# Gated linear attentions on one Trainium2 core: queries of all heads decayed in one VectorE operation, level products as matmuls of each head's own rows

## The chip, the cores and the metric

The kernel runs on one core of a Trainium2 chip. The metric is device time in microseconds (us) of one execution. Engines are called PE (TensorE), DVE (VectorE), ACT (ScalarE), POOL (GpSimd) and SP (the queue that issues DMAs).

## The reference

The program is a forward pass of a small network over one sequence of 512 tokens of width 1024: two layers that each run four token mixers side by side, then one layer of each of two other kinds. The mixers that matter here are two gated linear attentions, "hgrn" (4 heads of 64 key channels) and "gla" (4 heads of 32), both of this function, in chunks of 64 tokens:

```
def chunk_gla(q, k, v, log_f):
    ...
    bc = jnp.cumsum(gc, axis=3)                    # decay, summed inside the chunk
    def step(state, inp):
        q_, k_, v_, b_ = inp
        diff = b_[:, :, :, None, :] - b_[:, :, None, :, :]
        decay = jnp.where(causal, jnp.exp(jnp.where(causal, diff, 0.0)), 0.0)
        attn = jnp.einsum('bhid,bhjd,bhijd->bhij', q_, k_, decay)
        ...
        o = (jnp.einsum('bhij,bhjv->bhiv', attn, v_)
             + jnp.einsum('bhid,bhdv->bhiv', q_ * jnp.exp(b_), state))
```

The decay differs from channel to channel, so `attn` is no plain product of q and k. The kernel builds it by levels: for m = 32, 16, 8, 4, 2, 1 a chunk falls into blocks of 2m tokens, and the pairs whose key lies in the lower half and whose query in the upper half of one block are a plain product, once both are decayed to the border between the halves. Each pair belongs to one level; the diagonal is done apart.

## The kernel before

`Net` records every operation of every engine through one helper, so each instruction in the trace has the line of that helper, L328, and is told apart by its tiles. The program is written as generators. `merge` (line 656) and `project` (891) interleave them: in each of the two layers (`layer1`, 1898) one stream carries the projections of the four mixers and of the memory's keys and values, and the mixers' cores (`gdn` 1536, `hgrn_core` 1241, `gla_mix` 1274, the latent attention "mla" 1396 to 1480) start inside it as their inputs come. Then `Plan` (from line 265) orders each engine's instructions anew. It is a list scheduler with prices (`cost`, 330), waits between engines and tile buffers that come free; what it writes is the fixed order of every queue. A change in one operation therefore also moves others. Tiles in PSUM have names of three kinds: psA (3 buffers, projections), psS (3 buffers, for nearly everything small: scores, transposes, states, level products) and psD (2 buffers). In SBUF, p4w is the ring of sixteen 128x1024 work tiles, p4p the mixers' inputs, "p" or p2 the ring of 128x512 tiles; wh and wl are the two halves of a split weight.

`gla_core` (1074) computes either linear attention. Channels lie on partitions: hgrn has W = 1024 columns, two heads on 128 partitions and two such sets (hp = 2, n2 = 2), gla W = 512 and four heads of 32 partitions (hp = 4, n2 = 1). For each level `decays(m)` (1093) makes E: two DVE subtractions of the summed decay, one Exp on ACT, one DVE multiplication of the lower halves by k, 128 rows at once. The queries go elsewhere, into Q, which has a 32-column block for each head: line r of the loop multiplies only head r's partitions into head r's block, the rest of Q is zero (two Q buffers, cleared on POOL at lines 1112 to 1114):

```
for r in range(hp):
    self.mul(Q[rows(r), :, r, :]..., g(E)[rows(r), :, :, 1, :], g(q)[rows(r), :, :, 1, :])
```

The product of a level (1159 to 1167) then takes one matmul for a chunk and set: stationary E, 128 channels by 64 keys, moving Q, 64 columns (hgrn) or 128 (gla). All go to one psS tile, and one `copy_predicated` of DVE writes the level's entries from it into AT. Six levels, then the products with the state and with v, and `finish` (1044): norm, gate, and transposes into the operand of the output projection.

Of the kernel before, what the change touches and what calls it, by code (L numbers as in the profile page):

```python
# [12 lines left out]
U32 = mybir.dt.uint32  # L13
# [6 lines left out]
S = 512  # L20
# [10 lines left out]
LEVELS = (32, 16, 8, 4, 2, 1)  # L31
# [582 lines left out]
class Net:  # L614
# [459 lines left out]
    def gla_core(self, q, k, b, v, dk, scale, out):  # L1074


        W = q.shape[1]
        n2 = W // S
        hp = 128 // dk
        ns = NT * n2  # L1080
        bv = lambda t, m: t.rearrange("p (x two m) -> p x two m", two=2, m=m)
        AT = self.p4()
        vv = v.rearrange("p (t h d) -> p t h d", t=NT, h=4)
        rows = lambda r: slice(r * dk, r * dk + dk)
        prow = lambda c: slice((c % 2) * 64, (c % 2) * 64 + 64)
        fcol = lambda j, c: slice(j * S + c * 64, j * S + c * 64 + 64)


        scol = lambda c, j: slice(((c // 2) * n2 + j) * 64, ((c // 2) * n2 + j) * 64 + 64)
        a3 = lambda t: t.rearrange("p (a d) -> p a d", d=64)  # L1090
        big = lambda: self.p4() if n2 == 2 else self.p2()

        def decays(m):


            E = big()
            bb, ee = bv(b, m), bv(E, m)
            ref = bb[:, :, 0, m - 1:m].broadcast_to([128, W // (2 * m), m])
            self.sub(ee[:, :, 0, :], ref, bb[:, :, 0, :])
            self.sub(ee[:, :, 1, :], bb[:, :, 1, :], ref)  # L1100
            self.act(E, E, AF.Exp)
            self.mul(ee[:, :, 0, :], ee[:, :, 0, :], bv(k, m)[:, :, 0, :])
            Q = Qs[len(done) % 2]
            done.append(m)
            g = lambda t: t.rearrange("p (g x two m) -> p g x two m", two=2, m=m, g=nc8)
            for r in range(hp):
                self.mul(Q[rows(r), :, r, :].rearrange("p g (x m) -> p g x m", m=m), g(E)[rows(r), :, :, 1, :],
                         g(q)[rows(r), :, :, 1, :])
            return E, Q

        nc8 = n2 * 8
        Qs, done = [self.p4([128, nc8, hp, 32]) for _ in range(2)], []
        for Q in Qs:
            self.G.memset(Q, 0.0)

        kd = big()
        b3 = b.rearrange("p (c j) -> p c j", j=64)
        self.sub(kd.rearrange("p (c j) -> p c j", j=64), b3[:, :, 63:64].broadcast_to([128, nc8, 64]), b3)
        self.act(kd, kd, AF.Exp)
        self.mul(kd, kd, k)  # L1120
        qk = big()
        self.mul(qk, q, k, self.G)
        el = self.st([128, nc8])
        self.act(el, b3[:, :, 63], AF.Exp)
        yield self.when(kd)
        kdt = self.p4([128, n2, NT, 128])
        for j in range(n2):
            ps = self.ps("S")
            for t in range(NT):
                self.tr(ps[:, t * 128:(t + 1) * 128], kd[:, j * S + t * 128:j * S + (t + 1) * 128])  # L1130
            self.act(kdt[:, j].rearrange("p t c -> p (t c)"), ps, AF.Copy)
        E, Q = decays(LEVELS[0])
        yield self.when(kdt, qk)

        ps = self.ps("S")
        for t in range(NT):
            for j in range(n2):
                self.mm(ps[:, (t * n2 + j) * hp:(t * n2 + j + 1) * hp],
                        qk[:, j * S + t * 128:j * S + (t + 1) * 128], self.heads[dk])
        dg = self.st([128, 16])  # L1140
        self.act(dg, ps[:, 0:16], AF.Copy)
        St = self.p4([128, 8, n2, 64])
        self.V.memset(St[:, 0], 0.0)

        us = [self.ps("S", [128, ns * 64]) for _ in range(2)]
        for c2 in range(4):
            for j in range(n2):
                for c in (2 * c2, 2 * c2 + 1):
                    for r in range(hp):
                        self.mm(us[c % 2][rows(r), scol(c, j)], kdt[prow(c), j, c // 2, r * dk:(r + 1) * dk],  # L1150
                                vv[prow(c), c // 2, j * hp + r, :])
        for c in range(7):
            for j in range(n2):
                self.stt(St[:, c + 1, j, :], St[:, c, j, :], el[:, j * 8 + c:j * 8 + c + 1],
                         us[c % 2][:, scol(c, j)], ALU.mult, ALU.add)
        diag = self.K["lev"][:, 6 * 64:7 * 64].unsqueeze(1).broadcast_to([128, 16, 64])
        self.mul(a3(AT), diag, dg.unsqueeze(2).broadcast_to([128, 16, 64]), self.G)
        yield self.when(E, Q)
        for li, m in enumerate(LEVELS):
            ps = self.ps("S")  # L1160
            for c in range(8):
                for j in range(n2):
                    o0 = ((c // 2) * n2 + j) * hp * 32
                    self.mm(ps[prow(c), o0:o0 + hp * 32], E[:, fcol(j, c)], Q[:, j * 8 + c].rearrange("p r q -> p (r q)"))
            up = lambda t: t.rearrange("p (a x two m) -> p a x two m", two=2, m=m, x=32 // m)[:, :, :, 1, :]
            mask = up(self.K["lev"][:, li * 64:(li + 1) * 64].bitcast(U32)).broadcast_to([128, 16, 32 // m, m])
            self.V.copy_predicated(up(AT), mask, ps.rearrange("p (a x m) -> p a x m", m=m, x=32 // m))
            if li + 1 < len(LEVELS):
                E, Q = decays(LEVELS[li + 1])
            else:  # L1170
                E = big()
                self.act(E, b, AF.Exp)
                self.mul(E, E, q)
            yield self.when(E)
        o = self.p4()
        ov = o.rearrange("p (a r d) -> p r a d", r=hp, d=64)
        for r0 in range(0, hp, 2):
            pss = [self.ps("S", [128, ns * 64]) for _ in range(2)]
            for c2 in range(4):
                for j in range(n2):  # L1180
                    for c in (2 * c2, 2 * c2 + 1):
                        for i in range(2):
                            self.mm(pss[i][prow(c), scol(c, j)], E[rows(r0 + i), fcol(j, c)], St[rows(r0 + i), c, j, :])
            for i in range(2):
                self.act(ov[:, r0 + i], a3(pss[i]), AF.Copy, scale=scale)
        for half in range(2):
            ps = self.ps("S")
            for c2 in range(half * 2, half * 2 + 2):
                for h in range(4):
                    for c in (2 * c2, 2 * c2 + 1):  # L1190
                        a0 = (c2 * 4 + h) * 64
                        o0 = ((c2 - half * 2) * 4 + h) * 64
                        self.mm(ps[prow(c), o0:o0 + 64], AT[prow(c), a0:a0 + 64], vv[prow(c), c2, h, :])
            s = slice(half * 512, half * 512 + 512)
            self.stt(o[:, s], ps, scale, o[:, s], ALU.mult, ALU.add)
        out.append(o)
# [1323 lines left out]
```

## Time and profile before

| | |
|---|---|
| runs | 2051.95, 2046.83, 2048.59 us; median 2048.59 |
| profiled execution | 2043.82 us, span 2042.0 us, mean granted PE clock 0.989 |
| busy, share of the span | PE 96%, PE weight loads 81%, DVE 62%, ACT 47%, POOL 17% |
| PE records | 13254 (a float32 matmul leaves two, a float32r one or a transpose one) |
| the two mixer stretches | 107 to 310 us and 820 to 1035 us |

A duration in the rows is that of one instruction from its start to its end, and PE's matmuls overlap; what a matmul costs PE is the distance from one start to the next. A row of a timeline joins neighbours of one kind: its count is of records, and the start of the next row less its own start is what the group took. The number in brackets at a row's end is the idle time ahead of it and what ended it.

### The profile page before, as it was taken

Reading aid. Unit: us, or ns where it says so; the run is one execution under the profiler, and the core shown is the slowest. Engines: PE = TensorE matmul, PEld = TensorE weight load, DVE = VectorE, ACT = ScalarE, POOL = GpSimd, SP = SyncE. Lnnn points to the kernel's source line nnn. Section 1 sums busy time; section 2 is a strip of 40 time slices with the busy share of each in tenths; the row PEclk is TensorE's granted clock in tenths of the full one; section 3 lists DMA queues with packets and bytes.
Section 4 is the critical chain, followed back from the end, with each engine's and each line's share of the span. In section 5 each row is a group of like instructions: output and inputs, shape, how many; then the busy total and the mean of one; then the engine's idle time right before and its main releaser. Section 6 shows DMA issues by size and latency. Waiting matters only on the chain.

```text
span 2042.0 us, 33217 instructions
## 1 busy us (share of the span) xinstructions
PE 1963.9 (96%) x13254; PEld 1663.4 (81%) x13254; DVE 1265.9 (62%) x2313; ACT 955.0 (47%) x1721; POOL 356.8 (17%) x403
## 2 busy tenths in 40 slices
PE   6999999999999999999999999999999999999999
PEld 5888778888888878787788888888899988888787
DVE  7697883644442266879836444422548886558796
ACT  5763363433332246633634333322446663457782
POOL 3312121100000023112203000000323331105131
PEclk9999999999999999999999999999999999999999
DMA  5321224433332433301344333325331213331121
GB/s 159 99 71 36 71 67 164 117 100 93 94 102 93 155 108 93 76 23 55 94 150 119 93 94 102 93 93 175 114 83 49 77 62 114 126 91 53 62 73 62
DMA packets 231305, 191.88 MB, mean 94 GB/s; under 512 B 22224, under 2 KB 201072, under 8 KB 231152
## 3 DMA queue, kind: packets, MB, share of 16 engines
q1 hardware_dynamic: 231152, 189.77, 30.4%
q8 instruction: 104, 1.70, 0.4%
q14 instruction: 49, 0.40, 0.1%
HBM read 174.54 MB, written 15.20 MB: 93 GB/s over the span
## 4 chain that ended last, share of the span: by engine, by line
PE 80%; DVE 11%; ACT 3%; issue 2%; POOL 2%; DMA 1%; SPq 1%; DVEq 0%; ACTq 0%; POOLq 0%
PE psA L328 59%; PE psS L328 12%; PE psD L328 9%; DVE p4w L328 7%; DVE wl L328 1%; POOL st L328 1%; DVE p L328 1%; DVE st L328 1%; ACT p4w L328 1%; DVE p4p L328 1%; SPq L328 1%; ACT wh L328 1%; DVE p4h L328 0%; DMA p4p<-in_x_dram 0%; ACT p L328 0%
## 5 line engine op out<-in xcount | busy, mean ns | idle before, releaser
L328 PE MATMUL psA<-p4h,wh 128*128 128x512 f32 (+1 forms) x2144 | 626.0, 376 | 4.0 <-ACT p4h L328 2.6
L328 DVE TENSOR_TENSOR wl<-wr,wh 128x1024 fp32r<-128x1024 f32 (+5 forms) x290 | 336.6, 1165 | 392.2 <-ACT wh L328 386.8
L328 ACT CAST wh<-wr 128x1024 fp32r<-128x1024 f32 (+6 forms) x304 | 299.0, 990 | 474.8 <-PE psA L328 283.8
L328 PEld LDWEIGHTS psA<-p4h,wh 128*128 128x128 f32 x2144 | 392.6, 190 | 83.2 <-ACT p4h L328 4.4
L328 PE MATMUL psA<-p4h,wl 128*128 128x512 f32 (+1 forms) x1072 | 403.2, 377 | 1.5 <-DVE wl L328 1.5
L328 PE MATMUL psA<-wh,p4h 128*128 128x256 f32 (+1 forms) x1792 | 353.0, 290 | 2.1 <-DVE p4h L328 1.7
L328 PEld LDWEIGHTS psA<-wh,p4h 128*128 128x128 f32 x1792 | 284.0, 190 | 6.6 <-DVE p4h L328 2.3
L328 PE MATMUL psA<-wl,p4h 128*128 128x256 f32 (+1 forms) x896 | 259.8, 290 | 0.0
L328 POOL TENSOR_SCALAR st<-st 128x1 f32<-128x1 f32 (+4 forms) x108 | 40.0, 370 | 1139.1 <-ACT p4w L328 781.4
L328 PEld LDWEIGHTS psA<-p4h,wl 128*128 128x128 f32 x1072 | 203.9, 190 | 35.5 <-DVE wl L328 1.7
L328 PEld LDWEIGHTS psA<-wl,p4h 128*128 128x128 f32 x896 | 170.5, 190 | 1.6
L328 PE MATMUL psA<-wh,p4w 128*128 128x512 f32 (+1 forms) x540 | 159.5, 368 | 0.0
L328 ACT ACTIVATE p<-p 128x512 f32<-128x512 f32 (+2 forms) x174 | 88.1, 526 | 107.1 <-DVE p L328 105.9
L328 POOL TENSOR_TENSOR st<-st,c 128x1 f32<-128x1 f32 (+4 forms) x106 | 113.9, 1077 | 7.5
L328 PEld LDWEIGHTS psA<-wh,p4w 128*128 128x128 f32 x540 | 96.5, 188 | 18.4 <-issue 0.7
L328 ACT ACTIVATE p4w<-psA 128x256 f32<-128x256 f32 (+5 forms) x138 | 61.6, 451 | 101.9 <-PE psA L328 100.9
L328 PE MATMUL psS<-p4w,p4w 128*64 128x64 f32 (+9 forms) x800 | 98.1, 283 | 7.4 <-DVE p4w L328 7.3
L328 PE MATMUL psS<-consts,p4w 128*128 128x128 f32 (+1 forms) x448 | 71.0, 293 | 34.4 <-DVE p4w L328 18.8
L328 PE MATMUL psA<-wl,p4w 128*128 128x512 f32 (+1 forms) x270 | 98.4, 365 | 0.0
L328 PE MATMUL psS<-wh,p4w 128*128 128x512 f32 x300 | 97.4, 395 | 0.0
L328 DVE TENSOR_TENSOR p<-psA,p 128x512 f32<-128x512 f32 x54 | 37.3, 690 | 95.7 <-PE psA L328 94.2
L328 PEld LDWEIGHTS psS<-consts,p4w 128*128 128x128 f32 x448 | 55.1, 154 | 44.4 <-DVE p4w L328 17.1
(228 smaller groups left out, 3242.5 us busy)
## 6 DMA issues: line engine op xcount, KB each, us to landing
wr<-in_w_in_dram SPq DMA_DIRECT2D x44, 512.0 KB, 3.8
wr<-in_ffn_w_gate_dram SPq DMA_DIRECT2D x44, 512.0 KB, 3.8
wr<-in_ffn_w_up_dram SPq DMA_DIRECT2D x44, 512.0 KB, 3.9
wr<-in_ffn_w_down_dram SPq DMA_DIRECT2D x44, 512.0 KB, 3.5
wr<-in_w_out_dram SPq DMA_DIRECT2D x16, 512.0 KB, 4.4
wr<-in_a_w_in_dram SPq DMA_DIRECT2D x16, 512.0 KB, 3.8
wr<-in_b_w_in_dram SPq DMA_DIRECT2D x16, 512.0 KB, 3.9
p4w<-xd SPq DMA_DIRECT2D x12, 512.0 KB, 4.8
```

The source lines that it names most:

```text
L328: op.fn(*op.args, **op.kw)
```

## The change

`decays` multiplies the queries in place: the upper halves of E get q as the lower ones get k, 128 rows at once. Q, its clearing and its two buffers go. The level product is now taken for each head from that head's own partitions of E: stationary 64 or 32 channels by 64 keys, moving the 32 queries. Two heads at a time write to two psS tiles, and each head has its own `copy_predicated`.

```
-            self.mul(ee[:, :, 0, :], ee[:, :, 0, :], bv(k, m)[:, :, 0, :])
-            Q = Qs[len(done) % 2]
-            ...
-            for r in range(hp):
-                self.mul(Q[rows(r), :, r, :]..., g(E)[rows(r), :, :, 1, :], g(q)[rows(r), :, :, 1, :])
-            return E, Q
+            for i, f in enumerate((k, q)):
+                self.mul(ee[:, :, i, :], ee[:, :, i, :], bv(f, m)[:, :, i, :])
+            return E
...
-        Qs, done = [self.p4([128, nc8, hp, 32]) for _ in range(2)], []
-        for Q in Qs:
-            self.G.memset(Q, 0.0)
...
-            ps = self.ps("S")
-            for c in range(8):
-                for j in range(n2):
-                    o0 = ((c // 2) * n2 + j) * hp * 32
-                    self.mm(ps[prow(c), o0:o0 + hp * 32], E[:, fcol(j, c)], Q[:, j * 8 + c].rearrange("p r q -> p (r q)"))
...
-            self.V.copy_predicated(up(AT), mask, ps.rearrange("p (a x m) -> p a x m", m=m, x=32 // m))
+            for r0 in range(0, hp, 2):
+                pss = [self.ps("S", [128, ns * 32]) for _ in range(2)]
+                for c2 in range(4):
+                    for j in range(n2):
+                        for c in (2 * c2, 2 * c2 + 1):
+                            for i in range(2):
+                                x0 = (c2 * n2 + j) * 32
+                                e = E[rows(r0 + i), fcol(j, c)]
+                                self.mm(pss[i][prow(c), x0:x0 + 32].rearrange("p (x m) -> p x m", m=m), e, bv(e, m)[:, :, 1, :])
+                ...
+                for i in range(2):
+                    self.V.copy_predicated(up(AT, hp)[:, r0 + i], mask, pss[i].rearrange("p (a x m) -> p a x m", m=m, x=32 // m))
```

In the whole program the matmuls go from 11528 to 12008 (level products from 288 to 768), DVE's multiplications from 1121 to 1073 tensor-tensor operations, its predicated copies from 24 to 72, POOL's clearings from 40 to 32. The order of PE is the same but for the two mixer stretches. Three places follow.

PE, layer 0, one level product of gla in the middle of the stretch, before. psS_361 is the product's tile, p4w_266 is Q, p2_350 is E; psA are projections (the latent attention's values and 128x256 ones of later mixers), psD the products of gdn:

```order
L328 MATMUL psA_359_454<-p4w_336_431,wl340_435 128x512
L328 MATMUL psD_351_446<-p4w_231_326,p4w_107_202 64x64
L328 MATMUL psS_361_456<-p4w_266_361,p2_350_445 64x128
L328 MATMUL psD_351_446<-p4w_231_326,p4w_107_202 64x64 x3
L328 MATMUL psS_361_456<-p4w_266_361,p2_350_445 64x128 x7
L328 MATMUL psA_399_494<-wh276_371,p4h_17_112 128x256
```

The same engine and mixer after the change, one level (p2_369 is E, both operands):

```order
L328 MATMUL psS_368_463<-p2_350_445 64x32 x5
L328 MATMUL psS_380_475<-p2_369_464 64x32
L328 MATMUL psS_381_476<-p2_369_464 64x32
...
L328 MATMUL psS_382_477<-p2_369_464 64x32 x4
L328 MATMUL psA_432_527<-wl279_374,p4h_17_112 128x256
L328 MATMUL psA_432_527<-wh278_373,p4h_21_116 128x256
L328 MATMUL psA_467_562<-wh275_370,p4h_14_109 128x256
...
L328 MATMUL psS_383_478<-p2_369_464 64x32 x4
L328 MATMUL psS_382_477<-p2_369_464 64x32
L328 MATMUL psS_383_478<-p2_369_464 64x32
```

Heads 0 and 1 alternate between psS_380 and psS_381; of heads 2 and 3 four products of psS_382 go alone, then sixteen projection matmuls, then psS_383 and the rest.

PE, layer 0, end of the mixers, before: psA_524 is the last projection of gla's gate, psS_525 and psS_547 scores of the latent attention, psD and the other psS transposes:

```order
L328 MATMUL psA_524_619<-wh397_492,p4h_21_116 128x256
L328 MATMUL psS_525_620<-p4w_355_450,p4w_353_448 128x384
L328 MATMUL psS_525_620<-c49_144,c48_143 128x128
L328 MATMUL psD_532_627<-consts1_96,p2_513_608 128x128
L328 MATMUL psS_547_642<-p4w_355_450,p4w_353_448 128x512
L328 MATMUL psS_547_642<-c49_144,c48_143 128x128
L328 MATMUL psD_552_647<-consts1_96,p2_520_615 128x128 x2
L328 MATMUL psS_553_648<-consts1_96,p4w_325_420 128x128 x4
L328 MATMUL psS_555_650<-consts1_96,p4w_325_420 128x128 x4
```

The same place after, from the gate's last matmul (psA_510) to the next scores (psS_523):

```order
L328 MATMUL psA_510_605<-wh429_524,p4h_21_116 128x256
L328 MATMUL psS_511_606<-consts1_96,p4w_324_419 128x128 x4
L328 MATMUL psS_513_608<-consts1_96,p4w_324_419 128x128 x4
L328 MATMUL psS_515_610<-p4w_374_469,p4w_372_467 128x256
L328 MATMUL psS_515_610<-c49_144,c48_143 128x128
L328 MATMUL psD_520_615<-consts1_96,p2_501_596 128x128 x4
L328 MATMUL psS_563_658<-consts1_96,p4w_544_639 128x128 x4
L328 MATMUL psD_494_589<-consts1_96,p4w_435_530 128x128 x4
L328 MATMUL psS_564_659<-consts1_96,p4w_544_639 128x128 x4
L328 MATMUL psD_496_591<-consts1_96,p4w_435_530 128x128 x4
L328 MATMUL psA_521_616<-p4w_489_584,p4w_375_470 64x512
...
L328 MATMUL psS_523_618<-p4w_374_469,p4w_372_467 128x384
```

Before, 11 instructions stood between the gate and psS_555; after, 38 stand between the gate and psS_523: 28 transposes, one score product with its mask and eight products with values. psS_523 is the first of them that needs the buffer of psS_515.

ACT at the same place, before:

```order
L328 ACTIVATE p4p_194_289<-psA_524_619 128x256
L328 ACT_TABLE_LOAD
L328 ACTIVATE p4p_194_289<-p4p_194_289 128x1024
L328 ACTIVATE p4w_530_625<-psD_552_647 128x2x128
L328 ACTIVATE p4w_554_649<-psS_553_648 128x512
L327 ACT_TABLE_LOAD
L328 ACTIVATE p2_528_623,st_529_624<-psS_525_620,st_527_622 128x384
```

And after:

```order
L328 ACTIVATE p4p_192_287<-psA_510_605 128x256
L328 ACTIVATE p4w_512_607<-psS_511_606 128x512
L328 ACTIVATE p4w_514_609<-psS_513_608 128x512
L328 ACT_TABLE_LOAD
L328 ACTIVATE p4p_192_287<-p4p_192_287 128x1024
L328 ACTIVATE p2_490_585<-psD_520_615 128x256
L328 ACTIVATE p4w_495_590<-psD_494_589 128x512
L328 ACTIVATE p4w_540_635<-psS_563_658 128x4x128
L328 ACTIVATE p4w_541_636<-psS_564_659 128x4x128
L327 ACT_TABLE_LOAD
L328 ACTIVATE p2_518_613,st_519_614<-psS_515_610,st_517_612 128x256
```

In both the gate's activation (two table loads around it) stands ahead of the softmax that frees the scores' psS tile; after the change five more evacuations stand in that row.

## Rows read from the trace of the kernel before

**Rows 1.** Busy time by stretch: window, length, PE, PEld, DVE, ACT, POOL busy (instructions), granted PE clock, DMA share, GB/s. The first two long ones are the mixers of layers 0 and 1; the short ones lie inside them.
```profile
107.00:310.00 203.00, 190.03 (x2242) 162.03 (x2243) 169.82 (x347) 101.19 (x197) 43.39 (x42) 0.97 0.23 66
820.00:1035.00 215.00, 200.33 (x2336) 170.45 (x2335) 176.99 (x366) 107.52 (x204) 43.81 (x44) 0.96 0.23 67
...
156.00:160.00 4.00, 3.97 (x50) 3.60 (x50) 1.74 (x3) 0.00 (x0) 0.00 (x0) 0.57 0.01 4
292.50:299.50 7.00, 5.96 (x28) 4.87 (x28) 5.67 (x11) 3.95 (x10) 0.63 (x1) 0.51 0.05 18
```
**Rows 2.** PE, timeline (start, duration, records): a level product of hgrn and what follows it.
```profile
141.04 1.20 PE L328 MATMUL psS<-p4w,p4w 128*64 128x64 f32 x32
142.17 0.38 PE L328 MATMUL psA<-wh,p4h 128*128 128x256 f32 x1
```
**Rows 3.** PE, timeline: a level product of gla, and what follows it.
```profile
210.74 1.09 PE L328 MATMUL psS<-p4w,p 128*64 128x128 f32 x16
211.76 0.44 PE L328 MATMUL psS<-consts,p4w 128*128 128x128 f32 x2
```
**Rows 4.** PE, timeline: products of two heads in turn, whose operands lie on different halves of the partitions and whose results go to two psS tiles (64 partitions each, the chunk states), and what follows; then the same with 32 partitions each.
```profile
147.22 1.09 PE L328 MATMUL psS<-p4p,p4w 64*64 64x64 f32 x58
148.13 0.24 PE L328 MATMUL psD<-p4w,p4w 64*64 64x64 f32 x1
...
231.28 0.58 PE L328 MATMUL psS<-p4w,p 32*64 32x64 f32 x24
```
**Rows 5.** PE, timeline: matmuls with few moving columns (2 columns against 128 stationary ones; 32 against 32), each with the row after it.
```profile
143.09 1.62 PE L328 MATMUL psS<-consts,p4w 128*128 128x2 f32 x14
144.64 0.33 PE L328 MATMUL psS<-p4p,p4w 64*64 64x64 f32 x4
...
166.53 0.88 PE L328 MATMUL psD<-p,p4w 32*32 32x32 f32 x42
167.33 0.69 PE L328 MATMUL psS<-p4w,p4w 128*64 128x64 f32 x14
```
**Rows 6.** DVE, groups by form (count, busy us, mean ns): the query multiplications of hgrn and of gla, the key multiplications of hgrn and of gla, the predicated copies, and three reductions of psS tiles of falling width.
```profile
L328 DVE TENSOR_TENSOR p4w<-p4w,p4p 64x512 f32<-64x512 f32 x24 | 19.7, 821 | 0.2
L328 DVE TENSOR_TENSOR p4w<-p,p4p 32x256 f32<-32x256 f32 x48 | 23.2, 483 | 0.7
L328 DVE TENSOR_TENSOR p4w<-p4w,p4p 128x512 f32<-128x512 f32 x12 | 12.3, 1029 | 3.5 <-ACT p4w L328 3.4
L328 DVE TENSOR_TENSOR p<-p,p4p 128x256 f32<-128x256 f32 x12 | 6.6, 560 | 1.4 <-ACT p L328 1.4
L328 DVE COPY_PREDICATED p4w<-consts,psS 128x512 f32<-128x512 uint32 x24 | 21.9, 911 | 1.1 <-PE psS L328 0.7
L328 DVE TENSOR_REDUCE st<-psS 128x1 f32<-128x512 f32 x20 | 13.4, 680 | 0.2 <-PE psS L328 0.2
L328 DVE TENSOR_REDUCE st<-psS 128x1 f32<-128x256 f32 x52 | 20.9, 415 | 0.9 <-PE psS L328 0.7
L328 DVE TENSOR_REDUCE st<-psS 128x1 f32<-128x128 f32 x20 | 5.4, 280 | 0.1
```
**Rows 7.** PE, timeline of both layers: the matmuls inside the mixers' cores ahead of which PE stood idle longest until DVE had written a p4w tile (idle time in brackets).
```profile
154.54 0.42 PE L328 MATMUL psS<-p4w,p4w 128*64 128x64 f32 x6 [2.40 <-DVE p4w L328]
156.03 1.08 PE L328 MATMUL psD<-p4w,p4w 64*64 64x64 f32 x16 [1.08 <-DVE p4w L328]
208.20 0.99 PE L328 MATMUL psS<-p4w,p4w 64*64 64x64 f32 x22 [1.51 <-DVE p4w L328]
875.52 0.42 PE L328 MATMUL psS<-p4w,p4w 128*64 128x64 f32 x6 [1.50 <-DVE p4w L328]
877.01 1.12 PE L328 MATMUL psD<-p4w,p4w 64*64 64x64 f32 x16 [1.07 <-DVE p4w L328]
930.35 2.25 PE L328 MATMUL psS<-p4w,p4w 64*64 64x64 f32 x57 [1.52 <-DVE p4w L328]
```
**Rows 8.** DVE, timeline: the predicated copy that follows the product of the third group.
```profile
212.63 0.71 DVE L328 COPY_PREDICATED p4w<-consts,psS 128x512 f32<-128x512 uint32 x1
```
**Rows 9.** PE, timeline: the end of the mixers of layer 0, from the scores after the last gate projection on.
```profile
286.81 0.81 PE L328 MATMUL psS<-p4w,p4w 96*128 96x384 f32 x2
292.25 0.78 PE L328 MATMUL psS<-consts,p4w 128*128 128x128 f32 x4 [2.87 <-DVE p4w L328]
293.50 1.97 PE L328 MATMUL psS<-consts,p4w 128*128 128x128 f32 x8 [0.48 <-ACT p L328]
296.03 1.76 PE L328 MATMUL psD<-consts,p 128*128 128x128 f32 x7 [0.56 <-DVE p L328]
...
299.21 1.83 PE L328 MATMUL psA<-p4w,p4w 128*64 128x512 f32 x8
300.87 0.82 PE L328 MATMUL psA<-p,p4w 128*64 128x256 f32 x8
```
**Rows 10.** ACT, timeline: the same place, from the evacuation of the gate's last projection over its activation to the next evacuations.
```profile
287.96 0.38 ACT L328 ACTIVATE p4p<-psA 128x256 f32<-128x256 f32 x1
288.36 1.28 ACT L328 ACT_TABLE_LOAD   x1
289.65 1.06 ACT L328 ACTIVATE p4p<-p4p 128x1024 f32<-128x1024 f32 x1
290.88 0.59 ACT L328 ACTIVATE p4w<-psS 128x512 fp32r<-128x512 f32 x1
```

More of the change, by code (lines that the diff above doesn't have):

```diff
@@ L1101, in decays @@
             self.act(E, E, AF.Exp)
-            self.mul(ee[:, :, 0, :], ee[:, :, 0, :], bv(k, m)[:, :, 0, :])
-            Q = Qs[len(done) % 2]
-            done.append(m)
-            g = lambda t: t.rearrange("p (g x two m) -> p g x two m", two=2, m=m, g=nc8)
-            for r in range(hp):
-                self.mul(Q[rows(r), :, r, :].rearrange("p g (x m) -> p g x m", m=m), g(E)[rows(r), :, :, 1, :],
-                         g(q)[rows(r), :, :, 1, :])
-            return E, Q
+            for i, f in enumerate((k, q)):
+                self.mul(ee[:, :, i, :], ee[:, :, i, :], bv(f, m)[:, :, i, :])
+            return E
         nc8 = n2 * 8
-        Qs, done = [self.p4([128, nc8, hp, 32]) for _ in range(2)], []
-        for Q in Qs:
-            self.G.memset(Q, 0.0)
         kd = big()
@@ L1131, in gla_core @@
             self.act(kdt[:, j].rearrange("p t c -> p (t c)"), ps, AF.Copy)
-        E, Q = decays(LEVELS[0])
+        E = decays(LEVELS[0])
         yield self.when(kdt, qk)
@@ L1157, in gla_core @@
         self.mul(a3(AT), diag, dg.unsqueeze(2).broadcast_to([128, 16, 64]), self.G)
-        yield self.when(E, Q)
+        yield self.when(E)
         for li, m in enumerate(LEVELS):
-            ps = self.ps("S")
-            for c in range(8):
-                for j in range(n2):
-                    o0 = ((c // 2) * n2 + j) * hp * 32
-                    self.mm(ps[prow(c), o0:o0 + hp * 32], E[:, fcol(j, c)], Q[:, j * 8 + c].rearrange("p r q -> p (r q)"))
-            up = lambda t: t.rearrange("p (a x two m) -> p a x two m", two=2, m=m, x=32 // m)[:, :, :, 1, :]
-            mask = up(self.K["lev"][:, li * 64:(li + 1) * 64].bitcast(U32)).broadcast_to([128, 16, 32 // m, m])
-            self.V.copy_predicated(up(AT), mask, ps.rearrange("p (a x m) -> p a x m", m=m, x=32 // m))
+            for r0 in range(0, hp, 2):
[7 more added lines that the diff above has]
+                                self.mm(pss[i][prow(c), x0:x0 + 32].rearrange("p (x m) -> p x m", m=m), e, bv(e, m)[:, :, 1, :])
+                up = lambda t, n: t.rearrange("p (a r x two m) -> p r a x two m", two=2, m=m, x=32 // m, r=n)[:, :, :, :, 1, :]
+                mask = up(self.K["lev"][:, li * 64:(li + 1) * 64].bitcast(U32), 1)[:, 0].broadcast_to([128, ns, 32 // m, m])
+                for i in range(2):
+                    self.V.copy_predicated(up(AT, hp)[:, r0 + i], mask, pss[i].rearrange("p (a x m) -> p a x m", m=m, x=32 // m))
             if li + 1 < len(LEVELS):
-                E, Q = decays(LEVELS[li + 1])
+                E = decays(LEVELS[li + 1])
             else:
```

## The prediction

> **What bounds the kernel now.** I read the busy time by stretch first, since the change touches only the two mixer stretches, and the shares of the whole span mix them with 1500 us of dense projections. In both stretches PE is the fullest engine, 190.0 of 203 us and 200.3 of 215 us; DVE has 169.8 and 177.0, ACT and POOL are far below [rows 1]. So a microsecond taken from DVE is worth something only where PE stood waiting for it, and a microsecond of PE work added costs nearly a whole one. What PE leaves unused there is 13 and 15 us of idle time. A second loss hides in busy time: in some short stretches the granted clock is at about half, the lower of its two levels, 0.57 for 4 us and 0.51 for 7 us [rows 1]; the first comes behind idle times of 2.40 and 1.08 us [rows 7], the second behind one of 2.87 us [rows 9]. Next I looked in the timeline for the waits behind PE's idle time. The six longest inside the cores end on a DVE write and come to 9.08 us, 4.99 in layer 0 and 4.09 in layer 1 [rows 7]. The other place is the end of the mixers, 3.91 us in layer 0 [rows 9], and there ACT is what is late: the gate's activation with its table loads stands ahead of the softmax [rows 10].
>
> **PE's products.** Before, a level of hgrn takes 1.13 us for 16 matmuls up to the next start [rows 2], and one of gla 1.02 us for 8 [rows 3]; each holds one change of operand shape. Products of two heads in turn go faster: 29 matmuls in 0.91 us, 31 ns each, because two that read different partitions and write different psS tiles run side by side [rows 4]; those of 32 partitions, 12 in 0.58 us, are no slower than singles. I set a slot, one matmul or one such pair, at 60 ns, below 71 and 63 (the two groups of 64 columns divided out, with the change of shape still in them), and a change of shape at 0.1 us, between the 0.17 and 0.04 that then remain. Gla's old product is (1.02 - 0.1)/8 = 115 ns. Old products: 192 x 60 + 96 x 115 ns = 22.6 us. In the new order of PE I count, of 768 products, 284 neighbouring pairs and 200 that stand alone: 484 slots x 60 ns = 29.0 us. That is +6.4 us. Changes of operand shape along PE's order fall from 282 to 255: -2.7 us. Net **+3.7 us**.
>
> The new product has only 32 columns, and no row shows 64 stationary by 32 moving. Ends: if a slot fell to what 32 by 32 takes, (0.80 - 0.1)/21 = 33 ns [rows 5], 484 slots make 16.0 us, net -9.3; if nothing ran side by side, 768 x 60 ns = 46.1 us, net +20.8. I take 60, since the row with 2 columns on 128 stationary ones shows that few columns alone do not make a matmul cheap: 7 matmuls in 1.55 us, 221 ns each [rows 5].
>
> A rule speaks against many small matmuls. The row shows 58 records starting in 0.91 us, 16 ns apart [rows 4], so 1536 records are not held back by their number, and the sum stays. The Trainium skill, "TensorE: Matmul & The Clock Gate", section "Wait — 56ns, not 53.3ns?", states that starts are never closer than about 25 ns however few the columns; by it the sum would have 1536 x 25 ns = 38.4 us for the new products, 9.4 us more, and a time of 2055; here the trace disagrees and decides, so this gets no chance of its own.
>
> **DVE and POOL.** Removed: 24 query multiplications of 64 rows and 48 of 32 rows, 19.7 + 23.2 = 42.9 us. Added: 12 and 12 of 128 rows, priced as the key multiplications of the same shapes, 12.3 + 6.6 = 18.9 us. The copies go from 24 to 24 of half and 48 of a quarter of the width. Scaled by the reductions of psS tiles (680, 415, 280 ns): 24 x 911 x 415/680 + 48 x 911 x 280/680 = 13.3 + 18.0 = 31.3 instead of 21.9 us, +9.4 [rows 6]. DVE: -42.9 + 18.9 + 9.4 = -14.6 us, some 7 in each layer. It is worth at most the 9.08 us of PE's waits on DVE [rows 7] and at least nothing, since behind most of them stands a chain (subtraction, exponential on ACT, multiplication, matmul) of which the query multiplication is one link, and the copy, another link, gets more numerous. I take half, **-4.5 us**. POOL's eight clearings fall away; POOL is idle four fifths of these stretches [rows 1], so nothing. No DMA is added; SP's queue stays.
>
> **The end of the mixers.** The new order puts other work between the gate's last projection and the next scores, on both engines. PE: 28 transposes at 0.12 us (8 in 1.97 us at half clock [rows 9], halved) = 3.4, a score and its mask an estimated 0.4, eight products with values 1.2 (2.41 us for the two groups at half clock [rows 9], halved): 5.0 us. ACT until the scores' buffer is free, in the order shown: 0.38 + 2 x 0.59 + 1.28 + 1.06 + 0.38 + 3 x 0.59 + 1.28 + 0.4 = 7.7 us [rows 10]. So PE waits about 2.7 us instead of 3.91: -1.2. The lower clock costs 3.4 us there now (7 us at 0.51 [rows 1]). A wait of 2.7 us is nearer to the 2.87 than to the 2.40 that cost half as much, so I give back nothing. Both layers: **-2.4 us**. Ends: nothing, or the whole 7.3 us twice, -14.6, if the waits go and the clock holds, since 24 of the memory's projection matmuls that stood behind this place now stand among its scores.
>
> **The sum.** +3.7 - 4.5 - 2.4 = -3.2 us. The profiled execution would go from 2043.82 to 2040.6; it lies 4.8 us under the median of the runs, 2048.59, and on that scale I forecast **2045.4 us**. About 0.3%, 6 us, is what a measurement here can tell from no change, so that is within it.
>
> **Rivals.**
> 1. Faster, 2033 us. Either the end of the mixers closes up (-14.6 instead of -2.4) or the 32-column slot is as short as 32 by 32 (-9.3 instead of +3.7); each alone gives about -15. For it: the memory's projections that now stand among the scores, and a short slot for few columns in [rows 5]. Against: ACT's row of five more evacuations, and the 221 ns.
> 2. Slower, 2057 us: psS runs out. There are three buffers, a product now takes two of them until DVE has copied both, and the next pair can start in one only. The copy of the product in [rows 3] ended 1.58 us after the last matmul [rows 8]; a quarter as wide, 1.25. Four products alone, 0.24 us, cover little, so a boundary costs 1.0 us where nothing else stands between. There are 24 inside gla (one in a level, one between levels, two layers); half of them bare gives +12. Against: in the place shown sixteen projection matmuls stand between; it decides where less than about 1 us of other PE work does. DVE, full to 84% of these stretches, can make the lag longer.
> 3. Slower, 2062 us: two heads' products do not run side by side when 32 columns wide; +20.8 instead of +3.7.
> 4. The change doesn't do what it says: hardly possible for the instruction counts, which are fixed; what can fail is only that PE's waits follow DVE's time, and then the forecast loses its 4.5 us and stays within no change (2050).
>
> **How the numbers follow.** The forecast with its own spread (the half of the waits, rival 4) 0.42, rival 1 0.29, rival 2 0.22, rival 3 0.07. Of the first, 0.32 lies within 0.3%, 0.08 faster, 0.02 slower. So faster 0.37, same 0.32, slower 0.31. Cases of both signs hold more than half, so the range has to take in 2033 and 2057 with a little at both ends for their prices: 2030 to 2061. The forecast's own range is 2040 to 2050.
>
> **What would show it.** Right: level products in pairs, 32 records in about 0.5 us where uncut; DVE's busy time about 15 us lower; copies near 0.55 and 0.38 us; idle time ahead of the first level products halved; PE waiting 2 to 3 us behind the gate and the clock near half after it. Wrong: level products with idle time ahead of them ended by a DVE write of AT, psS short (rival 2); pairs at 120 ns (rival 3); slots of 33 ns or a full clock at the end of the mixers (rival 1).

## The result: slower by 1.1%

The changed kernel took 2067.76 us (median of six runs, 2061.43 to 2077.17), the kernel before 2046.62 in the same comparison: ratio 1.0107, 95% interval 1.0076 to 1.0137. The time lies above the range that was given, and on the other side of no change from the forecast. Its profiled execution took 2067.0 us.

The page of the changed kernel, span and busy time of each engine:
```profile
span 2065.2 us, 35119 instructions
PE 1980.0 (96%) x14214; PEld 1677.2 (81%) x14214; DVE 1255.6 (61%) x2313; ACT 953.5 (46%) x1721; POOL 351.9 (17%) x395
```
PE stands idle for 85.2 us of the span, where it was 78.1 (2042.0 - 1963.9). So 7 of the 23 us of added span are idle time, and 16 are "busy" ones. The granted clock by stretch shows where these are: first the two mixer stretches, moved to their new places, then three short ones inside the level products (columns as in [rows 1]):
```profile
105.10:323.00 217.90, 199.55 (x2726) 171.61 (x2727) 161.71 (x345) 100.04 (x197) 40.95 (x40) 0.92 0.20 57
834.80:1058.00 223.20, 203.30 (x2803) 172.69 (x2802) 167.21 (x362) 105.46 (x202) 40.52 (x42) 0.93 0.20 57
199.80:206.60 6.80, 6.04 (x51) 5.51 (x55) 3.86 (x7) 1.95 (x5) 0.00 (x0) 0.50 0.19 60
230.50:233.90 3.40, 3.40 (x25) 2.25 (x26) 2.65 (x6) 1.78 (x3) 0.00 (x0) 0.50 0.00 0
237.30:251.00 13.70, 13.70 (x138) 12.68 (x138) 4.16 (x12) 2.62 (x6) 0.00 (x0) 0.50 0.23 77
```
The mixers' mean clock was 0.97 and 0.96 and is 0.92 and 0.93. At half clock PE is busy without a gap, 13.70 of 13.70 us: nothing but the column of the clock tells that the time is lost there. Over the span the mean clock is 0.979 instead of 0.989.

The sum over all stretches that the trace gives at half clock, before and after:
```profile
sum 46.16, PE 40.93 PEld 36.54 DVE 34.64 ACT 18.08 POOL 9.29; mean PE 4.55 PEld 4.06 DVE 3.85 ACT 2.01 POOL 1.03
sum 87.12, PE 75.45 PEld 64.04 DVE 52.48 ACT 29.88 POOL 14.75; mean PE 5.39 PEld 4.57 DVE 3.75 ACT 2.13 POOL 1.05
```
PE was busy at half clock for 75.4 us instead of 40.9. What that costs I estimate from two groups of the same 32 records further below: 1.05 us from start to next start at full clock, 1.85 at half, so 43% of the busy time at half clock is lost. That is 15 us more. Together with 7 us of idle time it leaves 1 us of the 23 for PE's own work, where the forecast had 3.7.

In uncut pairs the level products go as expected where the clock holds. PE, timeline of the changed kernel: a piece of a level of hgrn with the row after it, then gla:
```profile
177.83 0.85 PE L328 MATMUL psS<-p4w 64*64 64x32 f32 x46
178.62 0.44 PE L328 MATMUL psA<-wh,p4h 128*128 128x384 f32 x1
...
227.89 0.67 PE L328 MATMUL psS<-p 32*64 32x32 f32 x32
229.44 0.42 PE L328 MATMUL psS<-p 32*64 32x32 f32 x8 [0.88 <-DVE p4w L328]
```
Twenty-three matmuls in 0.79 us with one change of shape, 34 ns each: two run side by side in a slot of 60. The last row shows the other loss: PE stands for 0.88 us until DVE has written p4w. DVE at that time:
```profile
229.09 0.29 DVE L328 COPY_PREDICATED p4w<-consts,psS 128x128 f32<-128x128 uint32 x1
```
The copy ends at 229.38, the product starts at 229.44. Gla's products read E, a "p" tile; the p4w tile is AT, and nothing but the psS buffer ties a product to a copy of other heads. PE by form, over the whole span:
```profile
L328 PE MATMUL psS<-p 32*64 32x32 f32 x768 | 25.6, 236 | 6.3 <-DVE p4w L328 6.0
L328 PE MATMUL psS<-p4w 64*64 64x32 f32 x768 | 24.3, 225 | 8.4 <-DVE p4w L328 8.4
```
14.4 us of waits on DVE ahead of level products. DVE did get its relief; by form, the in-place multiplications and the copies:
```profile
L328 DVE TENSOR_TENSOR p4w<-p4w,p4p 128x512 f32<-128x512 f32 x24 | 28.1, 1206 | 9.8 <-ACT p4w L328 9.8
L328 DVE COPY_PREDICATED p4w<-consts,psS 128x128 f32<-128x128 uint32 x48 | 13.9, 349 | 17.5 <-PE psS L328 17.2
L328 DVE COPY_PREDICATED p4w<-consts,psS 128x256 f32<-128x256 uint32 x24 | 11.6, 531 | 0.5 <-PE psS L328 0.4
L328 DVE TENSOR_TENSOR p<-p,p4p 128x256 f32<-128x256 f32 x24 | 9.4, 418 | 2.9 <-ACT p L328 2.9
```
The copies take 531 and 349 ns, by count and mean 29.5 us in all (forecast 31.3); DVE's busy time falls by 10.3 us. The kernel got no faster by it.

### The profile page after: what moved, and what is told of

Read it like the earlier page. It is cut to its first block, busy times and chain, and to the rows that moved or that the text cites. A ratio compares the mean times of both kernels' runs of the same rounds, so it can differ in the third digit from the quotient of the medians.

```text
span 2065.2 us, 35119 instructions
## 1 busy us (share of the span) xinstructions
PE 1980.0 (96%) x14214; PEld 1677.2 (81%) x14214; DVE 1255.6 (61%) x2313; ACT 953.5 (46%) x1721; POOL 351.9 (17%) x395
## 4 chain that ended last, share of the span: by engine, by line
PE 78%; DVE 12%; ACT 4%; issue 3%; POOL 3%; DMA 1%; SPq 0%; DVEq 0%; ACTq 0%; POOLq 0%
PE psA L328 57%; PE psS L328 12%; PE psD L328 9%; DVE p4w L328 6%; POOL st L328 2%; DVE p L328 1%; DVE wl L328 1%; ACT p4w L328 1%; DVE st L328 1%; DVE p4p L328 1%; ACT wh L328 1%; ACT p L328 1%; SPq L328 0%; DMA wr<-in_w_in_dram 0%; DVE p4h L328 0%
## 5 line engine op out<-in xcount | busy, mean ns | idle before, releaser
L328 PE MATMUL psA<-wh,p4h 128*128 128x256 f32 (+1 forms) x1792 | 358.3, 294 | 2.2 <-DVE p4h L328 1.8
L328 PEld LDWEIGHTS psA<-wh,p4h 128*128 128x128 f32 x1792 | 289.1, 193 | 6.9 <-DVE p4h L328 2.3
L328 PE MATMUL psS<-p4w,p4w 64*64 64x64 f32 (+8 forms) x416 | 80.1, 314 | 2.3 <-DVE p4w L328 1.0
```

The source lines that it names most:

```text
L328: op.fn(*op.args, **op.kw)
```

## The experiments

Theory C: the granted clock falls more often, because the products by heads leave most of the array empty. Theory O: `Plan` prices a product at 81 ns, 62 us for the 768, where those in uncut pairs take 34 ns each; the order built on this puts products ahead of what they need. Rival W: waits for psS buffers and copies by themselves. The table gives every run; clock is the range over a kernel's runs. The last two columns are of one execution, the profiled one: idle is span less PE's busy time, half is PE's busy time in all stretches at half clock. That execution can lie far from the median: in e11 it took 2057.67 us, in e10 2049.50, in e12 2037.24.

| run | what | us | ratio to before (95%) | clock | PE idle us | PE half us |
|---|---|---|---|---|---|---|
| before | | 2046.62 | 1 | 0.985 to 0.991 | 78.1 | 40.9 |
| the change | | 2067.76 | 1.0107 (1.0076 to 1.0137) | 0.972 to 0.984 | 85.2 | 75.4 |
| e1_hgrn_only | change in hgrn alone | 2053.91 | 1.0041 (1.0027 to 1.0055) | 0.983 to 0.987 | 89.1 | 60.7 |
| e2_gla_only | change in gla alone | 2101.68 | 1.0272 (1.0255 to 1.0289) | 0.970 to 0.975 | 99.7 | 94.5 |
| e3_wide | 64 columns | 2067.56 | 1.0112 (1.0093 to 1.0130) | 0.979 to 0.982 | 85.3 | 70.8 |
| e4_price | price 31 ns | 2053.51 | 1.0033 (1.0011 to 1.0056) | 0.975 to 0.991 | 70.9 | 79.7 |
| e5_before_price | before, its prices as measured | 2046.08 | 0.9994 (0.9986 to 1.0003) | 0.985 to 0.989 | 79.9 | 54.4 |
| e6_gla_price | gla alone, 31 ns | 2068.56 | 1.0104 (1.0089 to 1.0120) | 0.972 to 0.974 | 75.2 | 113.6 |
| e7_price_full | 31 ns, full products | 2032.81 | 0.9937 (0.9922 to 0.9952) | 0.989 to 0.991 | 68.3 | 29.7 |
| e8_price_diag | 31 ns, diagonal on DVE | 2060.87 | 1.0063 (1.0042 to 1.0085) | 0.971 to 0.980 | 65.6 | 97.8 |
| e9_full | full products, the changed kernel's order | 2060.72 | 1.0067 (1.0045 to 1.0089) | 0.982 to 0.987 | 90.2 | 54.3 |
| e10_price_wide | 31 ns, 64 columns | 2040.14 | 0.9979 (0.9954 to 1.0004) | 0.978 to 0.991 | 69.6 | 66.9 |
| e11_hgrn_price | hgrn alone, 31 ns | 2041.67 | 0.9988 (0.9970 to 1.0005) | 0.980 to 0.989 | 78.3 | 76.2 |
| e12_hgrn_price_wide | the same, 64 columns | 2042.33 | 0.9977 (0.9966 to 0.9989) | 0.986 to 0.990 | 75.1 | 37.2 |
| e13_before_thin | before, one head's partitions | 2047.55 | 1.0011 (0.9997 to 1.0025) | 0.981 to 0.985 | 74.3 | 62.5 |
| e14_price_time | 31 ns as a time only | 2052.83 | 1.0032 (1.0015 to 1.0048) | 0.978 to 0.984 | 74.6 | 79.4 |
| e15_price_dense | 31 ns for the sparse rule only | 2062.02 | 1.0081 (1.0065 to 1.0097) | 0.983 to 0.986 | 82.1 | 50.2 |

Idle time and the 43% of the half column give the spans of the table to within some 3 us; in e1, e2, e8 and e15 some 7 to 10 us are left open.

**The change by halves.** The edit of both is a branch on the number of heads on 128 partitions, `if hp == 2:` (e1) or `if hp == 4:` (e2) around the new decays and products, the old ones in the other branch.

> The change in hgrn alone; gla keeps Q and its products of 128 rows. Theory C (the granted clock of PE falls more often where gla's small products stand, and that is most of the loss): 2048 to 2054 us, 0 to 6 over the kernel before, since the two longest added stretches at half clock (13.7 us from 237 us on, 10.2 us from 971 on) lie in gla's levels and only one of 6.8 us in hgrn's. Rival W (waits for psS and for DVE's copies): also most in gla, whose level takes two pairs of tiles, so 2049 to 2055, but with the clock unchanged at 0.988 and idle time ahead of the level products of 5 us or more. Rival O (the planner's new order as such, wherever it is disturbed): about half the loss, 2057.

> The change in gla alone; hgrn keeps Q and its products of 128 rows. Theory C: 2058 to 2066 us, a mean granted clock near 0.981, half clock inside gla's levels. Rival W: the same time with the clock near 0.988. Rival O: about half the loss, 2057.

Hgrn's 2053.91 us lie inside what C and W gave, but they are 9 us over the kernel before in the same comparison, more than C's 6, and the clock fell, against W. Gla alone costs 57, more than both changes together: no theory had that, and it shows that the parts do not add. A planner that writes the whole order makes a new one of every edit, which is what O says, though not by the half that I had put on it. In gla alone the idle time and the busy time at half clock both grow, by 22 and 54 us.

**The price.**
```
# Plan.cost                                  (e4_price)
+            if self.level(op):
+                return 0.031
# Plan.order                                 (e14_price_time adds / e15_price_dense has instead)
+            if op.eng == "PE" and self.level(op):
+                op.dense = self.columns(op) / 81.0        # e15: / 31.0, and no change in cost
```


> The changed kernel with one number of the planner altered: a level product is priced at 31 ns, half the measured slot of a pair, instead of 81 ns; the order changes by some 40 rows of PE. Rival O (the planner keeps a wrong account of the time that lies between the products, so that copies and products meet too early): 2050 to 2058 us. Theories C and W: 2062 to 2070 us, little changed.

> The planner uses a product's price twice: as the time it takes, and, divided into its columns, to call it sparse and put it back while it wants dense work. Here only the time is 31 ns; for the second use the changed kernel's number stays. If the wrong time is what cost 14 us: 2050 to 2056 us as with the altered price. If the second use is: 2064 to 2070 us.

> The other half: the time stays 81 ns, and only for the sparse rule the product counts as with 31 ns (hgrn's products are then not put back any more). If the wrong time cost the 14 us: 2062 to 2070 us as the changed kernel. If the sparse rule did: 2050 to 2056 us.

One number of the planner is worth 14 us of the 21, the time alone 15, the sparse rule alone 6, all three by medians: the twelve runs of e4_price spread from 2033.55 us (clock 0.991) to 2061.25 (0.975). Of the changed kernel's profile to that of e4_price the span falls by 12.3 us and the idle time by 14.3, while the busy time at half clock does not (75.4 and 79.7 us): the price saved waits, not clock. That a truer price does it, and not just another order, is argued and not shown: all three kernels that got 31 ns gained (e4, e6, e11), but no other number was tried for these products. PE by form in e4_price:
```profile
L328 PE MATMUL psS<-p 32*64 32x32 f32 x768 | 26.2, 246 | 0.0
L328 PE MATMUL psS<-p4w 64*64 64x32 f32 x768 | 22.6, 235 | 7.0 <-DVE p4w L328 7.0
```
With the same three psS buffers and the same copies gla's waits are gone, 0.0 instead of 6.0 us: W is real in the changed order, but it comes from the order.

> Control for the run with the altered price: the kernel before, its level products priced at their measured slots, 58 ns in hgrn and 108 in gla, instead of 81 and 135. Theory O' (the changed kernel lost because the planner's account of its products, 62 us where they take 25 to 29, is much farther off than that of the old ones, 28 us where they take 22): 2040 to 2048 us, no change. Rival (any truer price gives the 14 us): 2031 to 2036 us.

> The change in gla alone, which took 2101.7 us, with the price of its level products at 31 ns. Theory O': most of the 57 us goes, 2045 to 2060 us. Rival (gla's products by heads are slow by themselves: tiles, copies, clock): 2080 us or more.

> The change in hgrn alone (2053.9 us) with its level products priced at 31 ns. Theory (order built on a wrong price): 2040 to 2048 us, idle time in the mixers no more than before. Rival: hgrn's loss is its pairs of tiles, 2052 to 2056 us.

The kernel before gains nothing from its measured prices, so they are no general cure. Gla alone gets back 33 of its 57 us and hgrn alone its whole loss. What is left in e6_gla_price, between the two numbers that I had set, is not waiting: PE idles 75.2 us there, less than before, at a clock of 0.972 to 0.974, and is busy at half clock for 113.6 us.

**The clock.** The products stream all 64 columns of a chunk (e3, e10, e12), and in e7 and e9 gla's also read 64 partitions. So e7 and e9 sum two heads in gla. In e13 the old products read one head's partitions, in the unchanged order of the kernel before, and the other heads' products are left out. Planner prices and columns are held at those of the kernel compared with:
```
# e3_wide, e10_price_wide, hgrn's in e12_hgrn_price_wide
-        self.mm(pss[i][prow(c), x0:x0 + 32].rearrange("p (x m) -> p x m", m=m), e, bv(e, m)[:, :, 1, :])
+        self.mm(pss[i][prow(c), x0:x0 + 64], e, e)        # x0 = (c2 * n2 + j) * 64
# e7_price_full, e9_full: as well
-        e = E[rows(r0 + i), fcol(j, c)]
+        e = E[i * 64:i * 64 + 64, fcol(j, c)]
# e13_before_thin
-        self.mm(ps[prow(c), o0:o0 + hp * 32], E[:, fcol(j, c)], Q[:, j * 8 + c]...)
+        self.mm(ps[prow(c), o0:o0 + hp * 32], E[rows(hp - 1), fcol(j, c)], Q[rows(hp - 1), j * 8 + c]...)
```


> The changed kernel, but each level product streams all 64 columns of its chunk instead of the 32 upper ones; the copies take the upper ones out of a psS tile twice as wide. Order of every engine and all prices of the planner are those of the changed kernel. If a slot is set by the 64 stationary columns, as I took it to be, the products take no longer, and PE streams twice the columns in the same time. Theory C: less time at half clock, mean clock 0.983 or more and 2058 to 2063 us. Rival W: nothing waits less, 2067 us as the changed kernel. If the slot is set by the moving columns instead: up to 484 x 30 ns = 15 us more, 2080 us.

> The run with the altered price again, same order and same prices on every engine, but each level product streams 64 columns and in gla reads 64 partitions instead of 32 (it sums two heads there, so gla's output is left wrong): per product up to four times the array work in the same slot. Theory C (after an idle stretch the clock stays at half for as long as the small products keep the array nearly empty): clock 0.985 or more, 2040 to 2046 us. Rival (the clock falls with the idle time alone, whatever the products do): clock 0.981 as in that run, 2052 us.

> The fuller products of the run e7_price_full (64 columns, 64 partitions in gla, which leaves gla's output wrong) in the order and at the prices of the changed kernel. If the two causes add (the clock held down by nearly empty products, and the order built on a wrong price), this lies as far under the changed kernel as that run lay under the one with the altered price: 2067 - 20 = 2047 us, clock 0.988 or more. If fuller products only help where the order leaves few waits: 2060 us or more, clock 0.982, since idle time in the cores remains.

e3_wide missed: twice the columns cost nothing, so the slot is not set by the moving columns, but they gave nothing either. e7_price_full is the clearest run of all. Two groups of hgrn's products, the last ahead of gla's, first in e4_price, then in e7_price_full, which have one order:
```profile
191.23 1.12 PE L328 MATMUL psS<-p4w 64*64 64x32 f32 x32
192.28 0.44 PE L328 MATMUL psA<-wh,p4h 128*128 128x384 f32 x1
...
196.83 1.92 PE L328 MATMUL psS<-p4w 64*64 64x32 f32 x32 [3.75 <-DVE p4w L328]
198.68 0.69 PE L328 MATMUL psA<-wh,p4h 128*128 128x384 f32 x1
```
```profile
191.48 1.15 PE L328 MATMUL psS<-p4w 64*64 64x64 f32 x32
192.56 0.44 PE L328 MATMUL psA<-wh,p4h 128*128 128x384 f32 x1
...
197.08 1.98 PE L328 MATMUL psS<-p4w 64*64 64x64 f32 x32 [3.73 <-DVE p4w L328]
```
With 32 columns the 16 products take 1.05 us up to the next start, with 64 columns 1.08; after the wait, at half clock, the first take 1.85. The busy time of the same stretch, e4_price and then e7_price_full:
```profile
193.00:212.00 19.00, 15.25 (x191) 13.78 (x191) 11.64 (x33) 5.48 (x15) 0.76 (x3) 0.55 0.12 36
```
```profile
193.00:212.00 19.00, 15.22 (x275) 13.63 (x275) 13.48 (x38) 6.98 (x17) 3.26 (x6) 0.82 0.22 64
```
Both begin with the same wait, and PE is busy as long. With the small products the mean clock is 0.55, with the fuller ones 0.82, and 275 records fit where 191 did. The clock falls inside the wait in both, and comes back after 17.1 us in one, after 6.8 in the other.

These are two executions, and the place alone doesn't prove the cause: in e8_price_diag (below), whose products are small too, half clock lasted 6.8 us here after a wait of 2.48. The runs as a whole do: the six of e7_price_full lie at clocks of 0.989 to 0.991 and 2031 to 2039 us; of the twelve of e4_price one came there (2033.55 us at 0.991), the rest lie at 0.986 and below. So small products make long stretches at half clock likelier, not certain. The medians differ by 20.7 us, 2053.51 and 2032.81. Of the two profiles the busy time at half clock differs by 50.0 us, by the 43% some 21 us of time, and the idle time by 2.6; their spans differ by 23.6. That leaves next to nothing for another rival, the changes of operand shape, of which gla's products on 64 partitions save some.

In the changed kernel's own order (e9_full) the same products bring 7 us, not 20: there PE waits 90 us, and the clock falls anew. So the two causes do not add; each hides part of the other.

> The kernel before in its own order on every engine, but each level product reads one head's partitions alone (64 in hgrn, 32 in gla, the last head; the other heads' products are left out of AT): the array is then as empty in a slot as under the changed products, and nothing else moves. Theory C: the clock falls more often where the level products stand, 0.981 to 0.985 and 2050 to 2058 us. Rival (the clock falls with idle time alone): 2046 us, clock 0.988.

Emptying the array in the old order brings the clock to 0.981 to 0.985 in its runs, with no wait added (74.3 us idle): C's clock, as expected. The time missed: 2 us, by the interval 5 at most, where 4 to 12 were expected. In its profile PE was busy at half clock for 62.5 us instead of 40.9, by the 43% some 9 us lost; 4 us less idle time stand against it, and some 3 us are left open.

> The run with the altered price, 64 columns streamed in both mixers but gla's products on 32 partitions as they are, so that all is computed rightly: a half of what e7_price_full added in gla. If columns and partitions count alike for the clock: between the two runs, 2040 to 2046 us, clock 0.985 to 0.988. If, as the run with 64 columns in the changed kernel's order suggests, columns alone give nothing: 2053 us, clock 0.980.

> The same, with 64 columns streamed in hgrn's products, all computed rightly and in the same order: hgrn's products then fill 64 partitions and 64 columns, gla's are the old ones. Theory C: the fastest right version, 2032 to 2042 us, clock 0.989 or more. Rival (the clock follows idle time alone): as the run before it.

With 64 columns and the price of 31 ns the whole result is computed, and both versions beat the changed kernel by over 25 us. The runs of e10_price_wide lie at 2034 to 2041 us with clocks of 0.987 and more and at 2047 to 2062 with 0.983 and less, so neither of its two expectations holds for all, and it is not surely faster than the kernel before. e12_hgrn_price_wide is, by 0.1 to 0.3%, just past the slow end of what was expected. It is the only version with the whole result whose interval lies under 1; those of e10 and e11 overlap with it, so what 64 columns add to e11 is not shown.

**POOL and DVE.** `self.mul(a3(AT), diag, ..., self.G)` without `self.G`, in e4_price.

> The run with the altered price, and the diagonal of AT multiplied on DVE instead of POOL. In the trace one subtraction of gla's first level takes 2.00 us on DVE instead of 0.42 while POOL's multiplication of 1.90 us runs, and PE then stands idle for 3.75 us in layer 0 and 3.24 in layer 1, ahead of 17 us at half clock. If DVE is held by POOL there: that subtraction at 0.42 us, idle time 2 us or less, 2040 to 2048 us. If it is the diagonal's own length that counts: 1.2 us more of DVE, no gain, 2052 us.

DVE and then POOL in the changed kernel, at the place of PE's wait that is the last row:
```profile
195.11 2.00 DVE L328 TENSOR_TENSOR p<-p 128x256 f32<-128x256 f32 x1
```
```profile
194.93 1.90 POOL L328 TENSOR_TENSOR p4w<-consts,st 128x1024 f32<-128x1024 f32 x1
```
```profile
200.56 1.28 PE L328 MATMUL psS<-p4w 64*64 64x32 f32 x20 [2.83 <-DVE p4w L328]
```
DVE in e8_price_diag, the same subtraction:
```profile
193.06 0.41 DVE L328 TENSOR_TENSOR p<-p 128x256 f32<-128x256 f32 x1
```
The hold is shown, 2.00 against 0.41 us, and the two waits fell, from 3.75 and 3.24 to 2.48 and 0.75 us, the first less than expected. The time rose by 7 us all the same, where a fall was expected, with the clock at 0.971 to 0.980 and 97.8 us of PE busy at half clock. Moving the diagonal made another order again, whose half-clock stretches, 17.1 and 20.5 us long, lie in gla. Why that order keeps the clock lower stays open.

Not tried: one psS tile for all heads, and a fourth psS buffer. So what psS by itself is worth, with no new order, is not measured.

## Why the prediction was wrong, point by point

- **The clock, the first of two steps that failed.** The forecast read the half clock as a thing that follows idle time at the end of the mixers, and asked only whether it stays there. The step "PE's products" priced slots and not what they leave of the array: gla's old products streamed 128 columns over 128 partitions in two slots of 60 ns, the new ones twice 32 columns over 32 partitions in one. No term and no rival had this. By the estimate above it is 15 of the 23 us of added span. Fuller products brought 20.7 us in the order with the altered price (e7_price_full) and 7.0 in the changed kernel's own order (e9_full), where waits bring the clock down as well.
- **PE's products.** Right: pairs run side by side at 60 ns (34 ns for each, a change of shape included), and 64 columns take no longer than 32, so the 60 rather than 33 was right. Net +3.7 forecast, about 1 left over in the balance, by an estimate that is good to some 3 us.
- **Waits, the second step that failed.** -4.5 us forecast; ahead of the level products they grew from 4.5 (3.9 in hgrn, 0.6 in gla, by the same view of the kernel before) to 14.4 us. The half that I took from DVE's relief needed the new order to meet DVE as the old one did. It is built on prices that I read, and I set the slots against each other only for the sum, not for where the products would stand. e4 and e14 show that this is what cost them: with the price of 31 ns the idle time falls by 14.3 and 10.6 us, and in e4 gla's waits on copies are gone.
- **Rival 2** (psS runs out, 12 us, 0.22) named the right mechanism: 6.0 us in gla end on a copy. It is half as large as priced, goes with the price of 31 ns, and is not the main loss.
- **DVE.** Copies 531 and 349 ns against 556 and 375. By counts and means the forms that were priced came to -15.4 us, near the -14.6: hgrn's in-place multiplications took 1206 ns and not 1029, gla's 418 and not 560. DVE's busy time fell by 10.3 all the same, since other operations on it took longer, as the subtraction held to 2.00 us.
- **The end of the mixers.** Forecast: a wait of 2.7 us and the clock kept low. The three waits now come to 4.68 us, where 3.91 stood [rows 9], and half clock still follows. PE of the changed kernel:
```profile
291.50 0.70 PE L328 MATMUL psS<-p4w,p4w 96*128 96x256 f32 x2 [0.62 <-ACT p L328]
...
295.94 1.11 PE L328 MATMUL psD<-consts,p4w 128*128 128x128 f32 x4 [2.29 <-DVE p4w L328]
298.83 1.12 PE L328 MATMUL psS<-consts,p4w 128*128 128x128 f32 x4 [1.77 <-DVE p4w L328]
```
  and ACT, where two weight casts that I had not counted stand ahead of the gate's evacuation at 291.35:
```profile
288.94 2.15 ACT L328 CAST wh<-wr 128x1024 fp32r<-128x1024 f32 x2
...
291.35 0.37 ACT L328 ACTIVATE p4p<-psA 128x256 f32<-128x256 f32 x1
...
292.72 1.28 ACT L328 ACT_TABLE_LOAD   x1
```
- **The rule on starts** of the Trainium skill, "TensorE: Matmul & The Clock Gate", section "Wait — 56ns, not 53.3ns?", that none are closer than about 25 ns: the row at 177.83 has 46 records starting in 0.79 us, 17 ns apart, so it did not hold here either, as the prediction had said.

## What to carry to other kernels

Price an edit of PE's work twice: by the time that its slots take, and by how much of the array it leaves empty, since PE was 100% busy at half its clock here for 13.7 us and only the granted clock said so. Where a planner with its own prices writes the order, check its price of the new operation against a row before anything else; here one such number held two thirds of the loss. And do not add causes that share a resource: the lower price gave 14 us, fuller products 7, both together 35.

## What the runs showed of the hardware that was not expected

- From inside a wait of 3.7 us on PE's clock stayed at half for 17.1 us where PE was given small products (32 or 64 partitions by 32 columns); in the same order with fuller ones it was back after 6.8 us (mean clock 0.55 against 0.82 over the 19 us). With small products it is not always so: one of twelve runs of e4_price held 0.991, as the six with fuller products did.
- 16 level products of 64 stationary columns take nearly the same time with 32 and with 64 moving ones (1.05 and 1.08 us; 2067.76 and 2067.56 us for the whole kernel, in one order).
- A subtraction of two SBUF operands on DVE took 2.00 us instead of 0.41 while POOL multiplied SBUF tiles for 1.90 us. The Trainium skill, "SBUF — State Buffer", section "Who interferes with whom", says that a DVE instruction with two SBUF inputs contends with a POOL instruction that reads SBUF, that the shared ports are an exclusive lock, and that the order of issue decides which of the two blocks; the trace agrees, the subtraction started 0.18 us after POOL's instruction and ended 0.28 us after its end.
